# A scheduling priority for the evictions of pair products in a two-layer trunk kernel

## The chip, the core and the metric

The kernel runs on one core of a Trainium2 chip. A core has a matrix engine (TensorE, PE in the profile; its weight loads are shown apart as PEld), a vector engine (VectorE, DVE), an activation engine (ScalarE, ACT), a general engine (GpSimd, POOL) and an engine that here only issues loads (SyncE, SP). TensorE writes its results to eight PSUM banks; VectorE and ScalarE read them from there ("evict" them) into SBUF. The metric is device time in microseconds; smaller is better.

## The reference

Two layers of a streaming-encoder block on a sequence of 512 frames of width 1024. Cut to what matters:

```python
for i in range(2):
    h = rmsnorm(x, norm1_g[i])
    z = h @ w_in[i] + b_in[i]            # q,k,v,o,i,f / rq,rk,rv,rg / two gates
    y_m = sigmoid(mo) * head_layernorm(mlstm(...))
    y_r = silu(rg) * head_layernorm(retention(rope(rq), rope(rk), rv))
    merged = sigmoid(gm) * (y_m @ w_bm[i]) + sigmoid(gr) * (y_r @ w_br[i])
    x = x + merged @ w_out[i]
    h2 = rmsnorm(x, norm2_g[i])
    x = x + square(relu(h2 @ w_ff1[i] + b_ff1[i])) @ w_ff2[i] + b_ff2[i]
    h3 = rmsnorm(x, norm3_g[i])
    x = x + sigmoid(h3 @ w_pe_gate[i]) * (p[i] @ w_pe[i])
return rmsnorm(x, final_g)
```

The line with `w_ff2` is the second half of the channel mix. Everything is float32.

## The kernel before

**Numbers.** Each float32 matrix product is done as three products of reduced-precision parts. A tensor is split into a high part (ScalarE copies it, line 286) and a low part (VectorE subtracts, line 287), and `mm3` multiplies high by high, high by low and low by high. The splits of weights are the largest single use of both engines.

**Units.** The weights come in units, in the fixed order of `unit_list`. A whole unit ("T8", "V", "PE") is one raw tile `wr` of 128 x 1024, split into `wh` and `wl`; `t8` runs 24 matmuls of 512 columns on it. A pair unit ("PAIR") covers a 1024 x 256 block of weights by a seven-product scheme: instead of eight quarter products there are seven, P1 to P7, each with 12 matmuls of 256 columns on sums of weights and sums of activations. `run_pair` emits them in the order P1, P5, P6, P2, P3, P7; P4 is put off and emitted after P1 and P5 of the next unit, or at another place that calls `flush`. The seven products read four pieces of weights: A (P1 and P5), B (P2 and P6), C (P3 and P7) and D (P4). Pieces are prepared in the order A, C, B, D, and sums in between them (lines 421 and 424) form what D needs. Three pieces of 128 x 1024 and two of D are held at once, and four raw tiles.

**Banks.** In a pair P1, P6, P7 and P4 write the same PSUM bank (named a), P2 its own (b), and P5 and P3 share one (c). Each product is evicted before the next one of its bank begins. So P6 waits for the eviction of P1, P7 for that of P6, P4 for that of P7, and P3 for that of P5.

**Evictions.** In `pair_tiles`, which serves the retention's q, k and gate tiles and two branch gates, ScalarE copies P1 (line 548), P5 (550), P6 (554) and P4 (560) to two tiles y, and VectorE adds P2 (552), P3 (556) and P7 (558) to them. After P4's eviction `consume(y)` applies what follows. In `ff2`, the second half of the channel mix, VectorE adds all seven products to the residual x (lines 1398 and 1400). Names of banks in the profile: l1o33a is layer 1, `ff2` of block 3, part 3, bank a; l0r2o0a is layer 0, retention head 2, gate tile pair 0; l0r1brqa the q of head 1; l0bgm2a a branch gate. A split of weights is wh_A, wl_A and so on by its piece, wh and wl for a whole unit.

**What sets the order.** The program is written for a scheduler. It numbers the instructions in the order in which the program emits them and then plays the program through with its own estimate of every duration. Whenever an engine is free on that clock, it takes, among the instructions that are ready, the one with the lowest number. What comes out is a fixed list for each engine, which the engine then runs in that order, waiting where something isn't there. All engines are ordered so, TensorE too. The splits alone have an order of their own: `in_order` ties each to the one before. A product's splits are emitted ahead of it by `ready`, as many as `READY` says, up to five pieces from the unit's first, and so reach into the next unit. A split that is emitted before an eviction has the lower number.

Of the kernel before, what the change touches and what calls it, by code (L numbers as in the profile page):

```python
# [38 lines left out]
OP = mybir.AluOpType  # L39
# [12 lines left out]
S = 256  # L52
UN = 1024
LOOK = 2
WARM = 11
NTMP = 6
RAWS = 4
# [178 lines left out]
def build(ctx, tc, ins, out):  # L236
    nc = tc.nc
    ve, ac, gp, te = nc.vector, nc.scalar, nc.gpsimd, nc.tensor
# [40 lines left out]
    def ps(name):  # L279
        return psum.tile([P, T], F32, name=name, tag="ps")  # L280

    def tmp(name, dt=F32):
        return cur["tmp"].tile([P, T], dt, name=name, tag="t", bufs=cur["ntmp"])
# [147 lines left out]
    def ready(k):  # L431
        while at["prep"] < min(len(order), k + 1):
            prep_next()

    def unit(kind):
        n = next_unit()
        assert units[n][0] == kind, (units[n], kind)
        ready(place[n, 0] + LOOK)
        return units[n], *pieces.pop((n, 0))
# [6 lines left out]
    def t8(act, name):  # L446

        _, wh, wl = unit("T8")
        o = ps(name)
        for k in range(KT):  # L450
            s = slice(k * P, (k + 1) * P)
            mm3(o, wh[:, s], wl[:, s], act[0][k], act[1][k], k == 0, k == KT - 1)
            if k == 3:
                flush()
        return o
# [16 lines left out]
    def run_pair(name, act, done):  # L472

        n = next_unit()
        assert units[n][0] == "PAIR", units[n]
        bank = {}

        def product(x):
            w, half, j = PRODUCTS[x]
            ready(place[n, "A"] + READY[x])  # L480
            wh, wl = [a[:, half * Q:(half + 1) * Q] for a in pieces[n, w]]
            b = {"P2": "b", "P5": "c", "P3": "c"}.get(x, "a")
            first = x in ("P1", "P2", "P5")
            if first:
                bank[b] = ps(f"{name}{b}")
            o = bank[b][:, 0:S]
            for k in range(4):
                s = slice(k * P, (k + 1) * P)
                h, l = act[k](j)
                f, e = first and k == 0, k == 3  # L490
                te.matmul(o, wh[:, s], h, start=f, stop=False, skip_group_check=True)
                te.matmul(o, wh[:, s], l, start=False, stop=False, skip_group_check=True)
                cur["mm"] = te.matmul(o, wl[:, s], h, start=False, stop=e, skip_group_check=True)
            done(x, o)

        def last():
            product("P4")
            for w in PIECE:
                del pieces[n, w]

        product("P1")
        product("P5")
        flush()
        for x in ("P6", "P2", "P3", "P7"):
            product(x)
        later.append(last)

    def run_wide(name, act, done, mid=None):
# [4 lines left out]
        for x, u in TURNS:  # L513
# [9 lines left out]
            if first and u == 0:  # L523
                bank[b] = [ps(f"{name}{b}{t}") for t in range(2)]
            ready(place[n, (y, u)] + LOOK)
            wh, wl = pieces.pop((n, (y, u)))
# [10 lines left out]
            if u:  # L537
                for t in range(2):
                    done(x, t, bank[b][t])

    def pair_tiles(name, act, consume, y=None):

        y = y or [tmp(f"{name}y{d}") for d in range(2)]
        a, b = slice(0, S), slice(S, T)

        def done(x, o):
            if x == "P1":
                ac.activation(y[0][:, b], o, AF.Copy)
            elif x == "P5":
                ac.activation(y[1][:, a], o, AF.Copy)  # L550
            elif x == "P2":
                ve.tensor_tensor(y[0][:, b], o, y[0][:, b], OP.add)
            elif x == "P6":
                ac.activation(y[1][:, b], o, AF.Copy)
            elif x == "P3":
                ve.tensor_tensor(y[1][:, b], o, y[1][:, b], OP.add)
            elif x == "P7":
                ve.tensor_tensor(y[1][:, a], o, y[1][:, a], OP.add)
            else:
                ac.activation(y[0][:, a], o, AF.Copy)  # L560
                consume(y)

        run_pair(name, act, done)

# [141 lines left out]
    def bcol(i, n, k):  # L706
        o, _ = _B[n]
        return bc[:, i, o + k:o + k + 1]
# [184 lines left out]
    def big(name, dt):  # L893

        return [bpool.tile([P, T], dt, name=f"{name}{k}", tag="big", bufs=KT) for k in range(KT)]

    x = big("x0", F32)
# [5 lines left out]
    warm = ps("warm")  # L903
    for _ in range(WARM):
        te.matmul(warm[:, 0:P], ones, ones, start=True, stop=True)
# [13 lines left out]
    for i in range(L):  # L919
# [132 lines left out]
        def r_qk(h):  # L1052
            nm = f"l{i}r{h}"
            qk = qk_tiles(nm)

            def rope(a, bn):
                b = [bcol(i, bn, 2 * h + d) for d in range(2)]

                def consume(y):

                    for d in range(2):
                        u = tmp(f"{nm}{bn}u{d}")
                        w = tmp(f"{nm}{bn}w{d}")
                        ve.scalar_tensor_tensor(u, y[0], b[0], trig[d], OP.add, OP.mult)
                        ve.scalar_tensor_tensor(w, y[1], b[1], trig[1 - d], OP.subtract, OP.mult)
                        ve.tensor_tensor(u, u, w, (OP.add, OP.subtract)[d])
                        split(u, qk[2 * a][d], qk[2 * a + 1][d])

                return consume

            for a, bn in ((0, "brq"), (1, "brk")):
                pair_tiles(f"{nm}{bn}", xs, rope(a, bn))
            return qk
# [17 lines left out]
        def r_gates(h, w, gs):  # L1091

            def consume(g):
                for d in range(2):
                    ac.activation(g[d], g[d], AF.Silu, bias=bcol(i, "brg", 4 * h + 2 * w + d), scale=SIGN[d])
                    gs[2 * w + d] = g[d]

            pair_tiles(f"l{i}r{h}o{w}", xs, consume)
# [14 lines left out]
        def gm_gates(p):  # L1113
            def consume(g):
                for d in range(2):
                    ac.activation(g[d], g[d], AF.Sigmoid, bias=bcol(i, "bgm", 2 * p + d), scale=SIGN[d])
                    gm[2 * p + d] = g[d]

            pair_tiles(f"l{i}bgm{p}", xs, consume)
# [84 lines left out]
        for d in range(4):  # L1204
            o = t8(xa, f"l{i}m0z{d}") if d else oz
# [92 lines left out]
        for c in range(KT):  # L1298
            o = t8(yr, f"l{i}br0{c}")
# [20 lines left out]
        for c in range(KT):  # L1320
# [6 lines left out]
            o = t8(yr, f"l{i}br1{c}")  # L1327
# [13 lines left out]
        if i == L - 1:  # L1341
            x_pool = phase("x", act_side)
            whole = x_pool.tile([P, KT, T], F32, name=f"l{i}x", tag="x")
            x = [whole[:, c, :] for c in range(KT)]
        else:
            x = big(f"l{i}x", F32)
# [4 lines left out]
        for c in range(KT):  # L1351
            o = t8((mh, ml), f"l{i}wo{c}")
# [35 lines left out]
        def tile3(c):  # L1388
            n3.tile(c, x[c])

        def ff2(b, p):
            started = set()

            def add(q, o, op):
                y = x[2 * p + q // 2][:, (q % 2) * S:(q % 2 + 1) * S]
                if b == 0 and q not in started:
                    started.add(q)
                    ve.scalar_tensor_tensor(y, y, bcol(i, "bf2", 2 * p + q // 2), o, OP.add, op)
                else:
                    ve.tensor_tensor(y, y, o, op)  # L1400

            def done(x_, o):
                if x_ in ("P1", "P2"):
                    add(1, o, OP.add)
                elif x_ == "P5":
                    add(2, o, OP.subtract)
                elif x_ in ("P6", "P3"):
                    add(3, o, OP.subtract)
                elif x_ == "P7":
                    add(2, o, OP.subtract)  # L1410
                elif x_ == "P4":
                    add(0, o, OP.add)
                    if b == 3 and p == 3:
                        tile3(6)
                        tile3(7)
                if b == 3 and p and x_ in ("P6", "P7"):
                    tile3(2 * p - 2 + (x_ == "P7"))

            def parts(k):
                h, l = hid[b, k]  # L1420
                return lambda j: (h[:, j * S:(j + 1) * S], l[:, j * S:(j + 1) * S])

            run_pair(f"l{i}o{b}{p}", [parts(k) for k in range(4)], done)
# [19 lines left out]
        for u in range(2):  # L1443
            _, wh, wl = unit("PE")
            for c in range(4):
                o = ps(f"l{i}pe{u}{c}")
# [33 lines left out]
        for c in range(KT - LAST if last else KT):  # L1480
            o = t8(n3.act, f"l{i}pg{c}")
# [44 lines left out]
    for a, n in enumerate(nn):  # L1526
        for c in range(KT - LAST, KT):
            _, wh, wl = ws[c - KT + LAST]
            o = ps(f"pl{a}{c}")[:, :256]
# [140 lines left out]
```

## Time and profile before

| what | value |
|---|---|
| median of 3 runs | 2348.01 us (2347.84 to 2348.44) |
| profiled execution | 2347.49 us |
| its span, first to last instruction | 2345.8 us |
| TensorE busy | 2320.2 us, 99% |
| VectorE busy | 1722.9 us, 73% |
| ScalarE busy | 1218.9 us, 52% |
| weight splits, low part, VectorE: wl_A, one of 76 | 1220 ns |
| mean granted TensorE clock | 0.997 of full speed |

How to read it: TensorE's matmuls overlap, and their ends are modelled, so its busy time has no gap even where it starts a matmul late by less than the length of one. Its pace is better read from the distance between the starts of neighbouring matmuls. An idle time in brackets in a timeline is that of the engine before the instruction, and the name behind the arrow is what ended it. In the waits, "PE l1o33a L491 <- DVE l1x L1400" reads: TensorE, about to write bank l1o33a at line 491, waited for the VectorE instruction of line 1400 that wrote l1x.

### The profile page before, as it was taken

Reading aid. Unit: us, or ns where it says so; the run is one execution under the profiler, and the core shown is the slowest. Engines: PE = TensorE matmul, PEld = TensorE weight load, DVE = VectorE, ACT = ScalarE, POOL = GpSimd, SP = SyncE. Lnnn points to the kernel's source line nnn. Section 1 sums busy time; section 2 is a strip of 40 time slices with the busy share of each in tenths; the row PEclk is TensorE's granted clock in tenths of the full one; section 3 lists DMA queues with packets and bytes.
Section 4 is the critical chain, followed back from the end, with each engine's and each line's share of the span. In section 5 each row is a group of like instructions: output and inputs, shape, how many; then the busy total and the mean of one; then the engine's idle time right before and its main releaser. Section 6 shows DMA issues by size and latency. Waiting matters only on the chain. (4 is left out here: it accounts for less than half of the span.)

```text
span 2345.8 us, 35261 instructions
## 1 busy us (share of the span) xinstructions
PE 2320.2 (99%) x13660; PEld 2056.2 (88%) x13660; DVE 1722.9 (73%) x2658; ACT 1218.9 (52%) x1768; POOL 245.7 (10%) x369
## 2 busy tenths in 40 slices
PE   9999999999999999999999999999999999999998
PEld 7888899898898898899888888998989988998997
DVE  7878767895675577677878787778958656776785
ACT  6656444553554445446557564454536445445454
POOL 3111101100102100000321110000000020000012
PEclk9999999999999999999999999999999999999999
DMA  5666676667578667676775645434343542433431
GB/s 201 187 180 172 218 229 170 205 189 202 168 230 269 195 198 189 199 219 181 206 221 169 182 124 186 136 126 158 108 158 104 166 153 96 130 108 98 132 117 59
DMA packets 146631, 394.89 MB, mean 168 GB/s; under 512 B 15376, under 2 KB 18832, under 8 KB 146464
## 3 DMA queue, kind: packets, MB, share of 16 engines
q1 hardware_dynamic: 99952, 247.77, 32.0%
q0 software_dynamic: 31104, 117.45, 20.4%
q10 hardware_dynamic: 15408, 27.43, 3.3%
q8 instruction: 107, 1.75, 0.3%
q14 instruction: 60, 0.49, 0.1%
HBM read 373.71 MB, written 123.73 MB: 212 GB/s over the span
## 5 line engine op out<-in xcount | busy, mean ns | idle before, releaser
L286 ACT ACTIVATE wh<-wr 128x1024 fp32r<-128x1024 f32 (+1 forms) x223 | 232.2, 1044 | 276.5 <-issue 69.6
L287 DVE TENSOR_TENSOR wl<-wr,wh 128x1024 fp32r<-128x1024 f32 (+1 forms) x221 | 271.9, 1232 | 77.7 <-ACT wh L286 77.5
L286 ACT ACTIVATE wh_B<-wr 128x1024 fp32r<-128x1024 f32 x100 | 105.9, 1059 | 159.2 <-PE l0f L443 8.5
L287 DVE TENSOR_TENSOR wl_B<-wr,wh_B 128x1024 fp32r<-128x1024 f32 x100 | 121.9, 1219 | 32.5 <-ACT wh_B L286 32.3
L286 ACT ACTIVATE wh_D<-wr 128x512 fp32r<-128x512 f32 x76 | 48.0, 632 | 124.9 <-DVE wr L424 65.4
L286 ACT ACTIVATE wh_C<-wr 128x1024 fp32r<-128x1024 f32 x76 | 80.2, 1056 | 61.3 <-issue 9.2
L286 ACT ACTIVATE wh_A<-wr 128x1024 fp32r<-128x1024 f32 x76 | 79.9, 1052 | 54.7 <-PE l1f L443 9.0
L287 DVE TENSOR_TENSOR wl_C<-wr,wh_C 128x1024 fp32r<-128x1024 f32 x76 | 94.3, 1240 | 18.7 <-ACT wh_C L286 18.5
L287 DVE TENSOR_TENSOR wl_A<-wr,wh_A 128x1024 fp32r<-128x1024 f32 x76 | 92.7, 1220 | 17.3 <-ACT wh_A L286 17.3
L442 PE MATMUL l1f<-l1n2h,wh 128*128 128x512 f32 x256 | 99.8, 390 | 0.0
L442 PE MATMUL l0f<-l0n2h,wh 128*128 128x512 f32 x256 | 99.8, 390 | 0.0
L444 PE MATMUL l0f<-l0n2h,wl 128*128 128x512 f32 x256 | 99.7, 389 | 0.0
L444 PE MATMUL l1f<-l1n2h,wl 128*128 128x512 f32 x256 | 99.7, 389 | 0.0
L443 PE MATMUL l1f<-l1n2l,wh 128*128 128x512 f32 x256 | 99.6, 389 | 0.0
L443 PE MATMUL l0f<-l0n2l,wh 128*128 128x512 f32 x256 | 99.6, 389 | 0.0
L287 DVE TENSOR_TENSOR wl_D<-wr,wh_D 128x512 fp32r<-128x512 f32 x76 | 52.4, 689 | 33.2 <-ACT wh_D L286 31.7
L421 DVE TENSOR_TENSOR wr<-wr,wr 128x512 f32<-128x512 f32 x76 | 52.1, 686 | 14.6 <-DMA wr<-wpairs 13.1
L444 PEld LDWEIGHTS l0f<-l0n2h,wl 128*128 128x128 f32 x256 | 48.0, 188 | 10.2
L444 PEld LDWEIGHTS l1f<-l1n2h,wl 128*128 128x128 f32 x256 | 48.1, 188 | 10.1
L443 PEld LDWEIGHTS l1f<-l1n2l,wh 128*128 128x128 f32 x256 | 48.1, 188 | 9.8
L442 PEld LDWEIGHTS l0f<-l0n2h,wh 128*128 128x128 f32 x256 | 48.1, 188 | 9.8
L442 PEld LDWEIGHTS l1f<-l1n2h,wh 128*128 128x128 f32 x256 | 48.1, 188 | 9.7
(5625 smaller groups left out, 8357.9 us busy)
## 6 DMA issues: line engine op xcount, KB each, us to landing
wr<-wstream SPq DMA_DIRECT2D x219, 512.0 KB, 4.2
wr<-wpairs SPq DMA_DIRECT2D x228, 256.0 KB, 2.8
wr<-wwide SPq DMA_DIRECT2D x24, 512.0 KB, 4.0
s0t<-wwide POOLq DMA_DIRECT2D x5, 1024.0 KB, 7.8
s4t<-wwide POOLq DMA_DIRECT2D x5, 1024.0 KB, 9.0
s12t<-wwide POOLq DMA_DIRECT2D x5, 1024.0 KB, 8.1
s16t<-wwide POOLq DMA_DIRECT2D x5, 1024.0 KB, 8.5
s1t<-wpairs POOLq DMA_DIRECT2D x4, 1024.0 KB, 6.7
```

What stands on the lines that cost most here:

```text
L286: a = ac.activation(hi_ap, src, AF.Copy)
L287: return a, ve.tensor_sub(lo_ap, src, hi_ap.bitcast(F32))
L421: ve.tensor_tensor(raws[n, "B"][:, Q:], kept.pop((n, "A"))[:, Q:], r[:, :Q], OP.add)
L442: te.matmul(o, sh, mh, start=first, stop=False)
L443: te.matmul(o, sh, ml, start=False, stop=False)
L444: cur["mm"] = te.matmul(o, sl, mh, start=False, stop=last)
```

## The change

`tc.high_priority(250)` is a context of the scheduler: instructions emitted inside it get a number that is lower by 250. The change puts the evictions of a pair's products inside such a context, in `pair_tiles` and in `ff2`. An eviction that is ready then comes before any ready instruction of the same engine that was emitted up to 250 instructions earlier, splits of weights among them. What follows an eviction, `consume(y)` and the norm's work, keeps its number. The instructions themselves and what they depend on are the same.

```diff
+AHEAD = 250
...
+    def ahead():
+
+        return tc.high_priority(AHEAD)
+
     def pair_tiles(name, act, consume, y=None):
...
         def done(x, o):
+            with ahead():
+                evict(x, o)
+            if x == "P4":
+                consume(y)
+
+        def evict(x, o):
             if x == "P1":
                 ac.activation(y[0][:, b], o, AF.Copy)
...
             else:
                 ac.activation(y[0][:, a], o, AF.Copy)
-                consume(y)
...
             def add(q, o, op):
                 y = x[2 * p + q // 2][:, (q % 2) * S:(q % 2 + 1) * S]
-                if b == 0 and q not in started:
-                    started.add(q)
-                    ve.scalar_tensor_tensor(y, y, bcol(i, "bf2", 2 * p + q // 2), o, OP.add, op)
-                else:
-                    ve.tensor_tensor(y, y, o, op)
+                with ahead():
+                    if b == 0 and q not in started:
+                        started.add(q)
+                        ve.scalar_tensor_tensor(y, y, bcol(i, "bf2", 2 * p + q // 2), o, OP.add, op)
+                    else:
+                        ve.tensor_tensor(y, y, o, op)
```

## The prediction

> **What bounds the kernel now.** I read the page first, then TensorE's waits, then the timelines of VectorE and ScalarE at the longest of them. Section 1 of the page:
>
> ```profile
> span 2345.8 us, 35261 instructions
> PE 2320.2 (99%) x13660; PEld 2056.2 (88%) x13660; DVE 1722.9 (73%) x2658; ACT 1218.9 (52%) x1768; POOL 245.7 (10%) x369
> ```
>
> TensorE is busy for all but 25.6 us of the span (2345.8 - 2320.2). The change touches no matmul, so about 1.1% is the most that any reordering of the other engines can show as idle time removed. The work is therefore to see which of those 25.6 us are waits for an eviction. TensorE's waits, longest first (who, for whom: us in total, times, longest):
>
> ```profile
> PE l0r2o1a L491 <- ACT wh_A L286: 3.4, 1, 3.4
> PE l1o33a L491 <- DVE l1x L1400: 1.6, 1, 1.6
> PE l0o33a L491 <- DVE l0x L1400: 1.3, 1, 1.3
> ...
> PE l0r0o0a L491 <- DVE l0r0o0y L558: 1.2, 1, 1.2
> PE l1r0o0a L491 <- DVE l1r0o0y L558: 1.2, 1, 1.2
> ...
> PE l0r1brqa L491 <- DVE l0r1brqy L558: 1.0, 1, 1.0
> ...
> PE l0o12a L491 <- DVE l0x L1400: 0.7, 1, 0.7
> ...
> PE l1r2o0a L491 <- ACT l1r2o0y L548: 0.5, 1, 0.5
> ...
> PE l0r2o0a L491 <- ACT l0r2o0y L548: 0.4, 1, 0.4
> ```
>
> Eight of these nine rows are released by one of the evictions that the change moves (L548, L558, L1400): 1.6 + 1.3 + 1.2 + 1.2 + 1.0 + 0.7 + 0.5 + 0.4 = 7.9 us. The largest is released by a split. So the profile has something for this change to win, but it is small: 7.9 us are 0.34% of 2348.0. I call 0.2% (4.7 us) the least that counts as a difference from no change.
>
> **The change, part by part.** It adds and removes no instruction, no DMA and no wait in the code; it gives the seven evictions of every pair a better place in the order in which VectorE and ScalarE take ready work. SyncE's loads and POOL's sums keep their places; a raw buffer comes free later only by as much as a split is delayed. A pair is 84 matmuls and 7 evictions, so 250 instructions reach back over two pairs, past every split that can still be open. On ScalarE, 52% busy, four evictions per pair also pass other activations; I cost that at nothing, since its idle half covers them.
>
> *P7's eviction before P4 (five places).* P4 writes the PSUM bank that P7's eviction reads. The worst place of its kind in layer 0, VectorE's rows and then TensorE's (start us, us, engine, line, operation; idle time before it in brackets):
>
> ```profile
> 412.74 1.22 DVE L287 TENSOR_TENSOR wl_A<-wr,wh_A 128x1024 fp32r<-128x1024 f32 x1
> 413.88 0.42 DVE L552 TENSOR_TENSOR l0r0o0y<-l0r0o0b,l0r0o0y 128x256 f32<-128x256 f32 x1
> 414.21 0.41 DVE L556 TENSOR_TENSOR l0r0o0y<-l0r0o0c,l0r0o0y 128x256 f32<-128x256 f32 x1
> 414.54 1.21 DVE L287 TENSOR_TENSOR wl_C<-wr,wh_C 128x1024 fp32r<-128x1024 f32 x1
> 415.67 0.42 DVE L558 TENSOR_TENSOR l0r0o0y<-l0r0o0a,l0r0o0y 128x256 f32<-128x256 f32 x1
> ...
> 414.74 0.28 PE L444 MATMUL l0r1s<-l0r1qh,l0r1kl 128*128 128x256 f32 x1
> 416.24 0.36 PE L491 MATMUL l0r0o0a<-l0xnh,wh_D 128*128 128x256 f32 x1 [1.22 <-DVE l0r0o0y L558]
> 416.43 0.28 PE L492 MATMUL l0r0o0a<-l0xnl,wh_D 128*128 128x256 f32 x1
> ```
>
> A split of 1.21 us (wl_C) stands directly ahead of the 0.42 us eviction for which TensorE is stopped. With the eviction first, it starts 1.13 us earlier (415.67 - 414.54) at the least, and more where it also passes wl_A. The loss at TensorE is larger than the wait: between starts lie 1.50 us where the neighbouring 256-column matmuls lie 0.12 apart, so 1.38, and the next distance is 0.19 instead of 0.12; together 1.45 for a wait of 1.22, or 0.23 more per place. Five waits of this kind (l1o33a, l0o33a, l0r0o0a, l1r0o0a, l0r1brqa) sum to 6.3 us, with 5 x 0.23 = 1.15 to 7.4 us. At l1o33a the blocker is of the same sort:
>
> ```profile
> 2282.96 1.99 DVE L287 TENSOR_TENSOR wl<-wr,wh 128x1024 fp32r<-128x1024 f32 x1
> 2284.88 0.41 DVE L1400 TENSOR_TENSOR l1x<-l1x,l1o33a 128x256 f32<-128x256 f32 x1
> ```
>
> The bounds are 0 (the eviction was not yet ready when the scheduler took the split) and 7.4; in the rows one split alone costs as much as the wait, so I take 7.3.
>
> *P1's eviction before P6 (two places, l0r2o0 and l1r2o0).* Here the eviction is ScalarE's, behind splits of the retention scores. Layer 0, where loads were late too; ScalarE's rows:
>
> ```profile
> 598.58 0.63 ACT L286 ACTIVATE l0r3vh<-l0r3vr 128x512 fp32r<-128x512 f32 x1 [2.83 <-DMA l0r3vr<-rv_spill]
> ...
> 602.69 1.04 ACT L286 ACTIVATE wh_A<-wr 128x1024 fp32r<-128x1024 f32 x1
> 604.01 1.03 ACT L286 ACTIVATE l0r3ph<-l0r3p 128x384 fp32r<-128x384 f32 x3 [0.28 <-DVE l0r3p L770]
> 604.95 0.36 ACT L548 ACTIVATE l0r2o0y<-l0r2o0a 128x256 f32<-128x256 f32 x1
> ```
>
> and three stretches of this place (TensorE, weight loads, VectorE, ScalarE, POOL busy with counts; granted clock; DMA share and GB/s):
>
> ```profile
> 600.40:603.70 3.30, 0.00 (x0) 0.00 (x0) 2.40 (x5) 2.45 (x4) 0.00 (x0) 0.81 1.01 398
> 603.70:609.40 5.70, 5.26 (x23) 4.97 (x24) 4.16 (x10) 2.89 (x8) 0.00 (x0) 0.51 0.35 113
> 609.40:620.00 10.60, 10.60 (x92) 10.60 (x91) 6.53 (x9) 6.17 (x11) 0.00 (x0) 1.00 0.34 106
> ```
>
> This is the kernel's only long stop: no matmul for 3.4 us, then 23 matmuls in 5.70 us at a granted clock of 0.51, which at the next stretch's pace (10.60 / 92 = 0.115 us) would have taken 2.65; so 3.4 + 3.05 = 6.4 us. TensorE had P6 of l0r2o0 left and lacked only P1's eviction for it; the scheduler, which orders TensorE's list too, had for that reason put the first matmuls of l0r2o1, with the late wh_A, ahead of P6. That eviction can pass at least wh_A and l0r3ph, 604.95 to 602.69, a gain of 2.3 us; the late load ahead of them (2.83 us) isn't touched. I take 2.1 here, with 0 and 6.4 as ends, and for layer 1 its wait of 0.5 with the 0.23 from above, 0.7. Together 2.8.
>
> The Trainium skill (TensorE: Matmul & The Clock Gate, Part 1, on the HAM clock gate) says that TensorE falls to half its clock after an idle window of about 3.4 us and needs about as long of steady work to come back. The row of 0.51 agrees. By that rule an eviction 2.3 us earlier would cut this stop below the window and save the slow stretch too, about 4.3 us for this place and 2338.8 in the end; I stay with 2.1, since only one such stop is in the trace.
>
> *P5's eviction before P3, channel mix (six places, o00, o10, o20 of both layers).* First and last of the six, TensorE's rows:
>
> ```profile
> 842.08 0.28 PE L493 MATMUL l0o00b<-l0hh,wl_B 128*128 128x256 f32 x1
> 842.37 0.38 PE L491 MATMUL l0o00c<-l0hh,wh_C 128*128 128x256 f32 x1
> ...
> 2166.05 0.28 PE L493 MATMUL l1o20b<-l1hh,wl_B 128*128 128x256 f32 x1
> 2166.36 0.39 PE L491 MATMUL l1o20c<-l1hh,wh_C 128*128 128x256 f32 x1
> ```
>
> Starts lie 0.29 and 0.31 us apart instead of 0.12, about 0.18 lost at each. I count this as 0, because of the next item: a microsecond later the same pairs hand over to a split that will be late.
>
> *The splits that are passed.* Every eviction moved ahead delays the splits behind it by 0.33 us (413.88 to 414.21 above). That is covered where the split is early. The tightest kind outside the channel mix is a whole unit like this one, which ends at 336.81 and is first read at 338.07, 1.26 us later, or three evictions:
>
> ```profile
> 335.60 1.21 DVE L287 TENSOR_TENSOR wl<-wr,wh 128x1024 fp32r<-128x1024 f32 x1
> ...
> 338.07 0.39 PE L444 MATMUL l0bm<-l0ymh,wl 128*128 128x512 f32 x1
> ```
>
> It is not covered for the first split of the second pair in a row in the channel mix (o01, o11, o21, both layers: six places). VectorE, then TensorE:
>
> ```profile
> 927.93 1.22 DVE L287 TENSOR_TENSOR wl_A<-wr,wh_A 128x1024 fp32r<-128x1024 f32 x1
> 929.07 0.41 DVE L1400 TENSOR_TENSOR l0x<-l0x,l0o10b 128x256 f32<-128x256 f32 x1
> 929.40 0.41 DVE L1400 TENSOR_TENSOR l0x<-l0x,l0o10c 128x256 f32<-128x256 f32 x1
> ...
> 929.20 0.38 PE L493 MATMUL l0o11a<-l0hh,wl_A 128*128 128x256 f32 x1
> ```
>
> The split ends at 929.15 and TensorE reads it 0.05 us later; two evictions that now come after it would come before it. Cost: 0 if neither was ready in time, 2 x 0.33 = 0.66 per place if both were, 0 to 4.0 us over six. P2's product (bank b) is older by one product than P3's (bank c), so one is nearly sure and the other open: I take 0.5 per place, 3.0 us.
>
> *l0o12a* (0.7) I leave as it is: its eviction stands behind a split that itself waited long for its data:
>
> ```profile
> 942.25 1.23 DVE L287 TENSOR_TENSOR wl_B<-wr,wh_B 128x1024 fp32r<-128x1024 f32 x1 [2.78 <-ACT wh_B L286]
> ```
>
> Sum: -7.3 - 2.8 + 3.0 = -7.1 us. The profiled execution took 2347.49 us, its span 2345.8 and 1.7 around it; the median of the three runs, 2348.01, is 0.5 above it. I put the sum on the median: **2341.0 us**, 0.30% faster.
>
> **The rivals.**
> *The priority finds little to pass.* The scheduler orders by its own clock. Where it believes that the split could start before the product was done, a better rank changes nothing, as at l0o12a, where VectorE stood 2.78 us at a split that the scheduler must have thought ready. For it also: l0r1brqa is waited for in layer 0 only, though both layers run the same code, so that wait hangs on how a load happened to land. Against it: at l0r0o0 VectorE was busy without a gap from 412.74 to 416, so split and eviction were both ready. Half of the 10.1 us won and the 3.0 paid leave 2.1: 2345.9 us, within 0.2%.
>
> *The queue behind an eviction stops.* VectorE and ScalarE run their lists in order. Where the scheduler's TensorE is ahead of the real one, P7's eviction stands at the head waiting for its product, and the next pair's wl_A behind it. That split would then end 0.41 + 1.22 = 1.6 us after P7, just when TensorE wants it. TensorE can start only the first matmuls of the next product meanwhile. Each pair so caught costs up to 1.6 us, and there are 76 pairs; 7.1 / 1.6, between four and five, eat the forecast's gain, and from eight on the kernel is slower by over 0.2%. With nine it comes to 2341.0 + 14.4 = 2355.4, which I take. For it: VectorE does already wait for products at evictions,
>
> ```profile
> DVE l1x L1400 <- PE l1o13a L493: 2.2, 2, 2.0
> ```
>
> Against it: a scheduler that takes only what is ready by its clock would have issued wl_A, which is ready before P7 ends, first. The Trainium skill (TensorE: Matmul & The Clock Gate, on the engine queue depths) calls the queues of ScalarE and VectorE strict FIFO; the split wl_B that held back a ready eviction at 942.25 agrees, and the rule speaks for this rival's mechanism without giving its size.
>
> **How the numbers follow.** Forecast 0.57: the blockers are seen in the rows, and small delays of splits are mostly covered. Little to pass: 0.25. A stopped queue: 0.18. So faster by over 0.2%: 0.57, within 0.2%: 0.25, slower: 0.18. The forecast's own range is 2334 (7.4 + 7.1 won, nothing paid) to 2343.3. The 8 in 10 range takes in the second case whole and the third up to nine caught pairs, 2334 to 2355.
>
> **What would show it.** Right: the five waits for L558 and L1400 gone from TensorE's waits; L548 of l1r2o0 ahead of the split l1r3ph; new or longer waits of 0.3 to 0.7 us for wl_A at o01, o11, o21; VectorE's and ScalarE's busy time and counts unchanged. Wrong: TensorE waiting for wl_A at many pairs; or the long stop near 600 us kept, moved, or doubled, since one such stop (6.4 us) is as large as the whole forecast.

## The result and the profile after

The changed kernel is slower: 2358.34 us median (2355.49 to 2362.18, five runs) against 2348.01 (2347.78 to 2349.22, five runs), a ratio of 1.0043 with an interval of 1.003 to 1.0056. The profiled execution took 2359.73 us. Section 1 of its page:

```profile
span 2358.0 us, 35261 instructions
PE 2324.5 (99%) x13660; PEld 2058.7 (87%) x13660; DVE 1723.5 (73%) x2658; ACT 1218.6 (52%) x1768; POOL 244.1 (10%) x369
```

Counts and busy times are those of before (VectorE 1723.5 for 1722.9, ScalarE 1218.6 for 1218.9); the span is 12.2 us longer. So no engine has more to do; something waits. In the changed file the lines of the prediction stand 1 to 11 lower: 287 and 288 are the splits, 422 and 425 the sums between pieces, 492 to 494 a pair's matmuls, 559, 561, 567 and 569 the evictions of `pair_tiles`, 1409 and 1411 those of `ff2`. TensorE's waits after (who, for whom: us in total, times, longest):

```profile
PE l0r2o1a L492 <- ACT wh_A L287: 3.4, 1, 3.4
PE l0o11a L492 <- DVE l0x L1411: 2.4, 2, 1.7
PE l0o02a L492 <- DVE l0x L1409: 2.3, 1, 2.3
PE l0o21a L492 <- DVE l0x L1411: 1.9, 2, 1.6
PE l0o33a L492 <- DVE l0x L1411: 1.7, 1, 1.7
PE l1o33a L492 <- DVE l1x L1411: 1.5, 1, 1.5
...
PE l0r1brqa L492 <- DVE l0r1brqy L569: 1.0, 1, 1.0
...
PE l1o11a L494 <- DVE wl_A L288: 0.8, 1, 0.8
PE l1o21a L494 <- DVE wl_A L288: 0.8, 1, 0.8
PE l0o11a L494 <- DVE wl_A L288: 0.8, 1, 0.8
PE l0o21a L494 <- DVE wl_A L288: 0.8, 1, 0.8
...
PE l1r0o0a L492 <- DVE l1r0o0y L569: 0.2, 1, 0.2
PE l0r0o0a L492 <- DVE l0r0o0y L569: 0.2, 1, 0.2
```

The reader is to see three things. The waits at r0o0 went from 1.2 to 0.2. Four waits of 0.8 for wl_A are new, as forecast. And three places that were not in the list before stand right behind its longest wait: l0o11, l0o02, l0o21, all in layer 0's channel mix, all waits for an eviction that was given priority.

Where the time came from shows best by stage. A stage here lasts from the first matmul of one bank's first tile to that of the next named one, in TensorE's timeline of one profiled execution each. The channel mix is the stretch from the first matmul of o00a to that of the next norm:

| stage | before | after |
|---|---|---|
| layer 0, pairs, l0r1brqa to the first of l0wo | 362.32 | 361.78 |
| layer 1, pairs, l1r1brqa to the first of l1wo | 355.18 | 354.21 |
| layer 0 channel mix, block 0 | 83.55 | 86.87 |
| block 1 | 84.57 | 87.87 |
| block 2 | 83.76 | 87.77 |
| block 3 to the norm | 47.06 | 47.59 |
| layer 0 channel mix, sum | 298.94 | 310.10 |
| layer 1 channel mix, sum | 296.97 | 299.66 |

Layer 0's channel mix loses 11.2 of the 12.2 us; layer 1's, the same code, 2.7; the two pair stages win 1.5. VectorE's waits within layer 0's channel mix name what is new, before and then after:

```profile
DVE wr L421 <- DMA wr<-wpairs: 4.1, 3, 1.8
```

```profile
DVE wr L422 <- DMA wr<-wpairs: 18.8, 8, 4.4
```

VectorE now stands for 18.8 us, eight times, at the sum of line 422, waiting for weights to land. (At the splits wl_B it stands less than before, 4.1 us for 8.9.) One such place in full, at the second pair of block 1. After the change, VectorE's timeline (start us, us, engine, line, operation; idle time before it in brackets) and TensorE's next row:

```profile
931.84 1.22 DVE L288 TENSOR_TENSOR wl_A<-wr,wh_A 128x1024 fp32r<-128x1024 f32 x1
...
941.40 0.69 DVE L422 TENSOR_TENSOR wr<-wr,wr 128x512 f32<-128x512 f32 x1 [3.79 <-DMA wr<-wpairs]
942.00 0.69 DVE L288 TENSOR_TENSOR wl_D<-wr,wh_D 128x512 fp32r<-128x512 f32 x1
942.61 0.41 DVE L1411 TENSOR_TENSOR l0x<-l0x,l0o11a 128x256 f32<-128x256 f32 x1
```

```profile
943.08 0.38 PE L492 MATMUL l0o11a<-l0hh,wh_C 128*128 128x256 f32 x1 [1.69 <-DVE l0x L1411]
```

Before, the same stretch of VectorE's list:

```profile
934.12 0.69 DVE L287 TENSOR_TENSOR wl_D<-wr,wh_D 128x512 fp32r<-128x512 f32 x1
934.81 0.42 DVE L1400 TENSOR_TENSOR l0x<-l0x,l0o11a 128x256 f32<-128x256 f32 x1
935.14 1.22 DVE L287 TENSOR_TENSOR wl_A<-wr,wh_A 128x1024 fp32r<-128x1024 f32 x1
...
936.61 0.68 DVE L421 TENSOR_TENSOR wr<-wr,wr 128x512 f32<-128x512 f32 x1
```

Two things differ. The sum now stands in the list ahead of wl_D and of the eviction of P6 (l0o11a), and what it reads isn't there for 3.79 us; before it stood behind both and behind wl_A, and did not wait. TensorE's P7 needs the bank that this P6 eviction empties, so it stops 1.69 us. The other two long waits are of the same kind: at 864.66 the sum waits 4.37 us ahead of the eviction for l0o02a, at 1029.20 it waits 3.72 ahead of that for l0o21a.

Why the weights are late: the load that lands last here was issued at 933.08 after, at 929.18 before. Loads issued in these narrow windows, with POOL's sum transfer (1024 KB) that was in flight beside them, KB each and us from issue to landing; after, then before:

```profile
s15t<-wpairs POOLq DMA_DIRECT2D x1, 1024.0 KB, 12.6
wr<-wpairs SPq DMA_DIRECT2D x1, 256.0 KB, 8.2
```

```profile
s15t<-wpairs POOLq DMA_DIRECT2D x1, 1024.0 KB, 11.6
wr<-wpairs SPq DMA_DIRECT2D x1, 256.0 KB, 2.8
```

And when POOL issued, after and then before:

```profile
932.32 0.91 POOL L332 DMA_DIRECT2D s15t<-wpairs  x1 [13.38 <-PE l0o10a L494]
```

```profile
929.30 0.91 POOL L331 DMA_DIRECT2D s15t<-wpairs  x1 [13.56 <-PE l0o10a L493]
```

Before, the load went out 0.12 us ahead of POOL's transfer and took 2.8 us. After, it went out 0.76 us behind it and took 8.2. Counted from the block's first matmul (920.01 before, 923.21 after) POOL issues at 9.3 and 9.1, so it is the load that moved, from 9.2 to 9.9. It is issued when its raw tile comes free: 0.02 to 0.03 us behind the end of the split wl_A of the pair o11 (start 927.93 in the rows of the prediction, 931.84 above, 1.22 us each). That split started 7.9 us into the block before and 8.6 after, so split and load moved by the same 0.7. Splits keep their order among themselves, and the one ahead of wl_A is piece D's: wl_D started at 926.05 before, 931.24 after, 6.0 and 8.0 us into the block, since l0hl, an eviction and other work now come ahead of it. Block 2 shows the same: the load behind its wl_A goes out 0.08 us ahead of POOL's transfer and takes 2.7 us before, 0.81 behind it and 8.2 us after. In block 0 the load that the sum waits for goes out 0.83 behind; there the sum stood ahead of the eviction before the change too, and only the load is new. Layer 1 has none of POOL's transfers in this stage, and its 42 loads there land in a median of 2.7 us in both kernels.

### The profile page after: what moved, and what is told of

Same layout as the page of the kernel before. It is cut to its first block, busy times and chain, and to the rows that moved or that the text cites. A ratio compares the mean times of both kernels' runs of the same rounds, so it can differ in the third digit from the quotient of the medians.

```text
span 2358.0 us, 35261 instructions
## 1 busy us (share of the span) xinstructions
PE 2324.5 (99%) x13660; PEld 2058.7 (87%) x13660; DVE 1723.5 (73%) x2658; ACT 1218.6 (52%) x1768; POOL 244.1 (10%) x369
## 3 DMA queue, kind: packets, MB, share of 16 engines
q0 software_dynamic: 31104, 117.45, 20.2%
## 4 chain that ended last, share of the span: by engine, by line
PE 87%; DVE 7%; DMA 2%; issue 2%; ACT 1%; POOL 0%; SPq 0%; DVEq 0%; ACTq 0%; POOLq 0%
PE l0f L443 2%; PE l1f L443 2%; PE l0f L444 2%; PE l1f L444 2%; PE l1f L445 2%; PE l0f L445 2%; DMA wr<-wpairs 1%; PE l0br L443 1%; PE l1br L443 1%; PE l1br L445 1%; PE l0br L444 1%; PE l1br L444 1%; PE l0br L445 1%; DVE wl_B L288 1%; PE l0bm L443 1%
## 5 line engine op out<-in xcount | busy, mean ns | idle before, releaser
L444 PEld LDWEIGHTS l0f<-l0n2l,wh 128*128 128x128 f32 x256 | 48.1, 188 | 9.7
```

The costliest lines, as they stand in the source:

```text
L444: te.matmul(o, sh, ml, start=False, stop=False)
```

## The experiments

Ratios are to the kernel before on the same chip, with 95% intervals. "Layer 0" is the sum of the four channel-mix stages of layer 0 in the profiled execution, worked out as above.

| kernel | median us | ratio | layer 0 |
|---|---|---|---|
| before | 2348.0 to 2349.7 | 1 | 298.9 |
| after | 2358.34 | 1.0043 [1.003, 1.0056] | 310.1 |
| e1_ff_only | 2361.27 | 1.0048 [1.0033, 1.0063] | 308.3 |
| e2_pairs_only | 2346.77 | 0.9988 [0.9979, 0.9997] | 298.5 |
| e3_no_sums_after | 2340.29 | 0.9956 [0.9941, 0.9971] | 299.6 |
| e4_no_sums_before | 2337.89 | 0.9945 [0.9928, 0.9961] | 298.5 |
| e5_sum_behind_C | 2370.81 | 1.0094 [1.0079, 1.0109] | 312.3 |
| e6_D_first_too | 2356.07 | 1.0035 [1.0022, 1.0048] | 305.4 |
| e8_sum_on_pool | 2362.40 | 1.0054 [1.0037, 1.0071] | 311.5 |
| e10_pairs_D_first | 2346.50 | 0.9988 [0.9979, 0.9998] | 298.7 |
| e11_after_sums_later | 2364.55 | 1.0065 [1.005, 1.008] | 317.7 |
| e13_before_sums_later | 2353.38 | 1.002 [1.0011, 1.003] | 306.1 |
| e15_before_sums_earlier | 2352.05 | 1.0014 [1.0005, 1.0024] | 300.6 |
| e14_D_chain_first | 2346.03 | 0.9988 [0.9978, 0.9997] | 299.6 |
| e16_D_chain_alone | 2347.87 | 0.9993 [0.9984, 1.0002] | 297.8 |
| e17_pairs_and_D_chain | 2345.42 | 0.9981 [0.9973, 0.999] | 298.0 |

### Which half of the change: e1 and e2

```diff
 # e1_ff_only, against after: pair_tiles as before
-            with ahead():
-                evict(x, o)
+            evict(x, o)
 # e2_pairs_only, against after: ff2 as before
-                with ahead():
-                    if b == 0 and q not in started:
+                if b == 0 and q not in started:
...
```

> Priority in ff2 alone, none in pair_tiles. Theory A (all of the loss lies in the channel mix: stage distances between the profiles before and after grow by 11.2 us in layer 0's channel mix and by 2.7 in layer 1's, while the pair stages shrink by 2.0): 2348.0 + 12 to 14 = 2360 to 2362, with a spread of some us from run to run. Rival (the changes of the pair stages shift when loads and sums collide later, so that the loss needs both): under 2355.

> Priority in pair_tiles alone, none in ff2. Theory A: the pair stages' gain without the loss, 2348.0 - 2.0 = 2346.0, 2345 to 2347, spread as small as before's 0.3 us. Rival (both parts needed): 2348 or more, or a spread of some us.

The loss is all with `ff2`: priority there alone gives 2361.27 and 308.3 us in layer 0's channel mix, priority in `pair_tiles` alone 2346.77 and 298.5. The pairs' half is worth about 3 us against before on the same chip (2349.72; 0.7 to 4.9 by the interval), not the seven that my forecast put on the whole.

### Are late loads the cause: e3 and e4

```diff
 # e3_no_sums_after on after, e4_no_sums_before on before, the same edit
-                sums[g, x] = tc.dram_tile([n, P, w], F32, name=f"s{index[g]}{x}")
+                pass
...
-        return given[g, x] if x in GIVEN else sums[g, x]
+        return given[g, x if x in GIVEN else {"t1": "B11", "t3": "B22", "t2": "B12"}[x]]
...
-        dma = gp.dma_start(flat(block(g, x)), flat(block(g, MADE[x][a])), max_dma_last_dim=4096, **kw)
-
-        tc.add_manual_dep(dma.ins, cur["mm"].ins.name, SYNC, reason="pace of the sums")
```

> The changed kernel without POOL's sums of weight blocks in DRAM: the loads that would read a sum read the first given block instead, so loads keep their number and size, the sums' own transfers are gone, and the output isn't the reference's. To be set against the next run. Theory B (layer 0 loses more than layer 1 because POOL's sums make its loads land late, and VectorE stands at the sum of line 422 with evictions queued behind): the loss against the same edit of the kernel before falls from 10 to 1 to 4 us, and layer 0's channel mix costs as much as layer 1's. Rival C (the new order itself costs it, whatever the loads do): the difference stays near 10 us.

> The kernel before with the same edit (no sums in DRAM, first given block read instead, output not the reference's); the baseline for the run before. Both theories: TensorE's long stop near 600 us may go too, since it waits for loads, so 2338 to 2348.

Without POOL's transfers the two lists differ by 2.4 us instead of 10.3, and by 1.2 in layer 0's channel mix instead of 11.2. So about nine tenths of that stage's loss need POOL's transfers. In e3 the pairs' loads of this stage land in a median of 2.9 us. These two runs take all of that traffic away; that it acts through late loads is for the runs below, which keep it. The change's own list has a remaining price of 1 to 2 us, which fits the four waits for wl_A.

### Moving the sum that stands: e5 and e8

```diff
 # e5_sum_behind_C, against after
-            ve.tensor_tensor(raws[n, "B"][:, Q:], kept.pop((n, "A"))[:, Q:], r[:, :Q], OP.add)
+            late = ve.tensor_tensor(raws[n, "B"][:, Q:], kept.pop((n, "A"))[:, Q:], r[:, :Q], OP.add)
+            tc.add_manual_dep(late.ins, cur["prep"][1].ins.name, ORDER, reason="sum behind the split of C")
 # e8_sum_on_pool, against after
-            ve.tensor_tensor(raws[n, "B"][:, Q:], kept.pop((n, "A"))[:, Q:], r[:, :Q], OP.add)
+            gp.tensor_tensor(raws[n, "B"][:, Q:], kept.pop((n, "A"))[:, Q:], r[:, :Q], OP.add)
```

> The changed kernel, with VectorE's sum of line 422 (which waits for the late load of a pair's piece B) tied behind the split of piece C in VectorE's list, so that fewer evictions and splits are queued behind it. Theory D (the place of the sum in the list is what hurts: VectorE stands at it 18.8 us in layer 0's channel mix, with ready evictions behind): most of the loss goes, 2358 falls to 2348 to 2351. Rival E (the load itself is late, because the splits that free its raw buffer are late; whatever waits for it, TensorE does in the end): 2355 or more, the wait moves to wl_B.

> The changed kernel with the sum of line 422 done by POOL instead of VectorE: nothing on VectorE's list waits for that load any more except the split wl_B. Theory D: the waits of TensorE for line 1411 in layer 0's channel mix go, 2348 to 2352, unless POOL's slower sum makes wl_B late. Rival E: wl_B is late instead, with the evictions queued behind it as before, 2355 or more.

Neither helps: e5 takes 2370.81 us and is slower than after, e8 takes 2362.40 and is level with it (the intervals overlap; 311.5 us in the stage for 310.1). If the sum's place in VectorE's list were the whole cause, taking it from there should have helped. It did not, because the late weights then stop the next instruction that needs them. VectorE in e8, where the sum has left the engine:

```profile
943.58 1.23 DVE L288 TENSOR_TENSOR wl_C<-wr,wh_C 128x1024 fp32r<-128x1024 f32 x1 [6.50 <-ACT wh_C L287]
944.72 0.42 DVE L1411 TENSOR_TENSOR l0x<-l0x,l0o11c 128x256 f32<-128x256 f32 x1
```

It stands 6.50 us at wl_C, again with evictions behind it. The first half of its load went out 0.80 us behind POOL's transfer and took 9.9 us. In e5 the same split waits, for 3.33 us, and the tile that the delayed sum still reads comes free later, so the next loads start later still: the one at this place goes out 3.4 us behind POOL's.

### Freeing D's raw tile: e6 and e10

```diff
 # e6_D_first_too on after, e10_pairs_D_first on e2_pairs_only
-            in_order("prep", *split(r[:, :w], *out_))
+            with ExitStack() as st:
+                if x == "D":
+                    st.enter_context(tc.high_priority(AHEAD))
+                in_order("prep", *split(r[:, :w], *out_))
```

> The changed kernel, with the split of piece D in the same priority context as the evictions, so that its raw buffer comes free earlier again (in the profile after, wl_D of the pair o10 of layer 0 starts 2.2 us later against the pair than in the profile before, and the next loads are issued right behind it). Rival E (late loads): most of the loss in layer 0 goes, 2349 to 2352. Theory D (place in the list): little changes, 2355 to 2360.

> Priority in pair_tiles and for the split of D, none in ff2. If late loads cost something in the kernel before too (rival E), this is faster than priority in pair_tiles alone: 2343 to 2346 beside its 2346.8. Theory D: the same as that run, 2346 to 2348.

D's split in the priority brings after from 310.1 to 305.4 in layer 0's channel mix; block 0 is back at 83.61, with no wait at that sum, blocks 1 and 2 are not (86.73 and 87.44). The whole time, 2356.07, can't be told from after's (the intervals overlap). At block 1 wl_D started 7.7 us into the block, hardly earlier than after's 8.0: the sum that forms D, line 425, kept its number and was itself passed by the evictions. wl_A started at 8.6, as in after, so the load went out 0.76 us behind POOL's transfer again and took 8.3 us. e10 shows that the same edit does no harm with the pairs' half (2346.50).

### Moving POOL's transfers: e11, e13 and e15

```diff
 # e11_after_sums_later on after, e13_before_sums_later on before
-        tick(units[n][0])
+        if units[n][0] != "PAIR":
+            tick(units[n][0])
...
+        tick("PAIR")
 # e15_before_sums_earlier, against before: paced by P3's last matmul, not P7's
-        tc.add_manual_dep(dma.ins, cur["mm"].ins.name, SYNC, reason="pace of the sums")
+        tc.add_manual_dep(dma.ins, cur.get("pace", cur["mm"]).ins.name, SYNC, reason="pace of the sums")
...
+            if x == "P3":
+                cur["pace"] = cur["mm"]
```

> The changed kernel with POOL's transfers for the sums of weight blocks let go one to two products later in each pair (after P5 and the put-off P4 of the pair instead of at its start), some 3 to 4 us. Theory F (the evictions delay the split that frees a raw buffer, the next load is issued 0.7 to 1.2 us later and so just behind the start of POOL's transfer, and lands after 6 to 8 us instead of 2.7): the load at 9.9 us after the block's start slips in front of the transfer again, the loss in layer 0's channel mix falls from 11 to 2 to 5 us, 2349 to 2353. Rival G (a late load costs wherever the transfer stands, since some load always meets it): 2356 or more.

> The kernel before with the same later sums; the control. Theory F: layer 0's channel mix as before or a little better, 2346 to 2350. Rival G: 2348 as well, but then the run above does not come near it.

> The kernel before, with no priority anywhere, and POOL's transfers for the sums let go one product earlier in each pair (at the end of P3 instead of P7, 1.4 us). Theory F: the load that is issued at 9.2 us after a block's start, 0.1 to 0.2 us ahead of the transfer, now comes behind it and lands late: layer 0's channel mix loses 5 to 12 us without any priority, 2353 to 2360, with some us from run to run. Rival H (the evictions' place in VectorE's list is needed for the loss): within 2 us of the kernel before.

e11 does not heal the change: 317.7 in the stage, with VectorE waiting 20.2 us at the sum. The load of the disputed place in block 1 (929.51) is ahead of POOL's transfer (934.04) again, takes 3.8 us, and nothing waits for it; but the load for the pair after it (935.27) goes out 1.23 behind and takes 7.8, and TensorE's long waits are now at l0o12 and l0o22 (3.2 and 3.1 us). Part of the 317.7 is another thing: the last block costs 54.63, and e13, which has the same later transfers and no priority, loses as much there (55.17 for 47.06). Its first three blocks are as before or better, so e13 says nothing on the disputed place. e15 is the useful one: it makes the late load meet a list without any priority. In block 1 the load issued at 933.30 goes out 1.2 us behind POOL's (932.13) and lands as late as after's:

```profile
wr<-wpairs SPq DMA_DIRECT2D x1, 256.0 KB, 7.6
```

VectorE in e15:

```profile
938.94 0.42 DVE L1404 TENSOR_TENSOR l0x<-l0x,l0o11a 128x256 f32<-128x256 f32 x1
939.28 1.22 DVE L287 TENSOR_TENSOR wl_A<-wr,wh_A 128x1024 fp32r<-128x1024 f32 x1
...
940.94 0.69 DVE L423 TENSOR_TENSOR wr<-wr,wr 128x512 f32<-128x512 f32 x1
943.54 1.23 DVE L287 TENSOR_TENSOR wl_C<-wr,wh_C 128x1024 fp32r<-128x1024 f32 x1 [1.91 <-ACT wh_C L286]
```

The eviction of l0o11a is done by 939.36, before the sum; the block takes 83.63 us. So a 7.6 us load costs nothing here, and the same holds in block 2 (7.8 us, 83.88). The stage as a whole is 1.6 us longer than before, and block 0 alone loses 1.9 (85.49 for 83.55). There the sum stands ahead of the eviction for l0o02a without any priority, in the list of before too (859.37 and 861.08, with no wait at the sum), and now its load is late:

```profile
865.59 0.69 DVE L423 TENSOR_TENSOR wr<-wr,wr 128x512 f32<-128x512 f32 x1 [3.97 <-DMA wr<-wpairs]
...
867.20 0.47 DVE L1402 SCALAR_TENSOR_TENSOR l0x<-l0x,bc,l0o02a 128x256 f32<-128x256 f32 x1
```

TensorE then waits 1.7 us for that eviction; after the change it waits 2.3 at the same place. With e3 this makes a table of two by two for layer 0's channel mix: a list without priority with loads on time 298.5 (e4), with late loads 300.6 (e15); after's list with loads on time 299.6 (e3), with late loads 310.1. The new list alone costs 1.2 us, the late loads alone nothing where the eviction stands ahead of the sum, the two together more than eleven. Theory F of the expectation, that the late load is enough, missed (2352.05, expected 2353 to 2360): the eviction must stand behind the sum as well.

### Undoing the cause inside the change: e14

```diff
 # e14_D_chain_first, against after: e6's edit, and the sum that forms D
-            ve.tensor_tensor(r[:, :Q], r[:, :Q], r[:, Q:], OP.add)
+            with tc.high_priority(AHEAD):
+                ve.tensor_tensor(r[:, :Q], r[:, :Q], r[:, Q:], OP.add)
```

> The changed kernel with the sum that forms piece D (line 425) and the split of D both in the priority context, so that their raw buffer comes free earlier than in the earlier run, which gave the split alone and moved it by 0.3 us only. Theory F: in blocks where the next loads get in front of POOL's transfer the loss goes, 2349 to 2354; the loss that is left is that of wl_A and of blocks where they don't. Rival H: 2356 or more in spite of earlier loads.

With both steps of D's chain in the priority the whole loss is gone: 2346.03, 299.6 in the stage. All evictions still have their priority. VectorE at the place shown above:

```profile
931.59 0.68 DVE L425 TENSOR_TENSOR wr<-wr,wr 128x512 f32<-128x512 f32 x1
...
932.79 0.41 DVE L1415 TENSOR_TENSOR l0x<-l0x,l0o11a 128x256 f32<-128x256 f32 x1
```

The sum (here line 425) still stands ahead of the eviction, as in after, but its load was issued at 925.70, 1.3 us ahead of POOL's (927.02), and landed in time:

```profile
wr<-wpairs SPq DMA_DIRECT2D x1, 256.0 KB, 2.7
```

The four waits for wl_A are gone too: at block 1 wl_A starts 6.5 us into the block, after's at 8.6. Late loads as such are not gone: VectorE still stands 10.6 us at this sum in the stage, six times, for 4.1 before. At 939.25 it stands 2.33 us there, and behind it TensorE waits 0.9 us at l0o12, where before, with VectorE 2.78 us at wl_B, it waited 0.7. So the length of VectorE's waiting is no measure of the loss.

### What the chain is worth by itself: e16 and e17

e16 is before with e14's two edits alone; e17 is e2 with them.

> Kernel before with one addition: the sum that forms D and D's split get the priority (250 instructions); no eviction has any. Theory (the loss came only from evictions passing D's chain in the channel mix, and an earlier D chain is worth something by itself because D's raw buffer comes free sooner): the block l0o10 is issued and costed as before or better, its four channel-mix stages of layer 0 sum to 297 to 300 us (298.9 before), time 2344 to 2349. Rival (what the two additions recovered in the earlier run needed the evictions ahead as well): the D chain now passes evictions of the channel mix that TensorE waits for, the four stages cost 2 to 6 us more than before, time 2350 to 2354.

> The priority for the pairs' evictions alone (none for the channel mix's sums), and for the sum that forms D and D's split. Theory: the pair stages give the 1 to 2 us that the priority gave there in every kernel that had it, and the D chain what it gives alone; so 1 to 2 us below the kernel with the D chain alone, 2343 to 2347. If the channel mix's priority is worth its name once the D chain is no longer passed, then the kernel with all three (2346.0) stands at least 1 us below this one; if it is worth nothing, this one is level with it or faster.

The chain alone is level with before (0.9993, the interval holds 1): its own worth is not shown, so e14's 3 us below before are not shown to come from it. e17 has the lowest median of the kernels that compute the reference (e3 and e4 don't), 2345.42, 4.2 us below before on its chip; it beats before and after, but its interval overlaps those of e2, e10 and e14. It has no priority in `ff2`, and e14, which has it, is not faster (2346.03). So the priority in `ff2` is worth nothing that can be measured, even where it does no harm.

## Why the prediction was wrong

Forecast 2341.0, in the range 2334 to 2355; the time is 2358.34, slower and outside.

**The step that failed** stands in one sentence of the change part by part: "a raw buffer comes free later only by as much as a split is delayed", costed at nothing. As far as it goes it held: in block 1 the split wl_A, which frees the raw tile, came 0.7 us later, and the load was issued 0.7 us later. What the step left out is that a load's landing is not its issue plus a constant: 0.7 us later meant behind POOL's transfer, and 8.2 us instead of 2.8. The prediction had listed POOL's queue and SyncE's as keeping their places, which they did; what changed was which of them came first. The second half of the error is the place of the line 422 sum. I looked at splits that evictions pass, and not at what then stands in front of the next eviction when loads are late. Together they make nearly 10 of the 11.2 us of layer 0's channel mix, by difference (1.9 are its two waits for wl_A, and 0.5 came back at P3; e3 and e4 also leave 1.2 of 11.2 without POOL's transfers), and nothing in the sum stood for them.

**P7's eviction before P4 (7.3 forecast).** The prediction calls l0r0o0 (1.2) the worst place of its kind in layer 0; by its own list that is l0o33a (1.3). It was right at l0r0o0 and l1r0o0: the eviction now stands ahead of wl_D and wl_A, and the wait is 0.2. VectorE after:

```profile
413.19 0.42 DVE L569 TENSOR_TENSOR l0r0o0y<-l0r0o0a,l0r0o0y 128x256 f32<-128x256 f32 x1
413.52 0.68 DVE L288 TENSOR_TENSOR wl_D<-wr,wh_D 128x512 fp32r<-128x512 f32 x1
```

Two of the 6.3 us of waits went. At l0r1brqa the 1.0 stayed: VectorE stood 3.68 us at the sum for a load, then ran wl_C, and only then the evictions.

```profile
385.17 0.69 DVE L422 TENSOR_TENSOR wr<-wr,wr 128x512 f32<-128x512 f32 x1 [3.68 <-DMA wr<-wpairs]
385.78 1.22 DVE L288 TENSOR_TENSOR wl_C<-wr,wh_C 128x1024 fp32r<-128x1024 f32 x1
...
387.25 0.42 DVE L569 TENSOR_TENSOR l0r1brqy<-l0r1brqa,l0r1brqy 128x256 f32<-128x256 f32 x1
```

At o33 of both layers they stayed too (1.7 and 1.5 for 1.3 and 1.6); a whole unit's wl is still directly ahead of the eviction. Layer 1, VectorE after:

```profile
2295.49 1.98 DVE L288 TENSOR_TENSOR wl<-wr,wh 128x1024 fp32r<-128x1024 f32 x1
2297.39 0.41 DVE L1411 TENSOR_TENSOR l1x<-l1x,l1o33a 128x256 f32<-128x256 f32 x1
```

The rival in which the priority finds little to pass holds at these three places: the list still puts a split first, so on the scheduler's clock the product was not done. That this is its reason was not tried.

**P1's eviction before P6 (2.8 forecast).** The long stop of layer 0 is kept: TensorE waits 3.44 us for wh_A, and the following 5.70 us run at a granted clock of 0.50. That stretch of after (TensorE, weight loads, VectorE, ScalarE, POOL busy with counts; granted clock; DMA share and GB/s):

```profile
603.55:609.25 5.70, 5.53 (x25) 5.38 (x26) 4.20 (x9) 3.03 (x8) 0.00 (x0) 0.50 0.34 123
```

ScalarE's list moved the eviction ahead of two of three pieces of l0r3ph and not ahead of wh_A, 604.38 for 604.95:

```profile
602.63 1.04 ACT L287 ACTIVATE wh_A<-wr 128x1024 fp32r<-128x1024 f32 x1
603.95 0.52 ACT L287 ACTIVATE l0r3ph<-l0r3p 128x384 fp32r<-128x384 f32 x1 [0.28 <-DVE l0r3p L780]
604.38 0.37 ACT L559 ACTIVATE l0r2o0y<-l0r2o0a 128x256 f32<-128x256 f32 x1
```

Of the 2.1 nothing came, since TensorE's list still has the matmul for wh_A first. In layer 1 the wait of 0.5 is gone. What a shorter stop would do to the clock stays open: in every run the stop is 3.4 to 3.8 us, or gone (e3, e4). The prediction's price for such a shorter stop does not add up either: 2.1 for the eviction and 3.05 for the slow stretch make 5.2 us and 2337.9, not 4.3 and 2338.8.

**wl_A delayed (3.0 forecast).** Right in mechanism, and near in size: at o11 and o21 of both layers, none at o01. TensorE at l1o11, after:

```profile
2096.72 0.28 PE L493 MATMUL l1o11c<-l1hl,wh_A 128*128 128x256 f32 x1
2097.77 0.39 PE L494 MATMUL l1o11a<-l1hh,wl_A 128*128 128x256 f32 x1 [0.77 <-DVE wl_A L288]
```

Starts lie 1.05 apart instead of 0.12, so 0.93 at each of four places, 3.7 us for 3.0.

**P5's eviction before P3 (0 forecast).** Won at all six places: starts lie 0.12 apart where they lay 0.29 to 0.31, about 0.18 each, 1.1 us. TensorE at the first of them, after:

```profile
841.95 0.28 PE L494 MATMUL l0o00b<-l0hh,wl_B 128*128 128x256 f32 x1
842.06 0.28 PE L492 MATMUL l0o00c<-l0hh,wh_C 128*128 128x256 f32 x1
```

**The slower rival** had the sign and half of the picture: VectorE's list does stop, and what TensorE needs stands behind. But what stands at the head is a sum that waits for a load, and what is held back is an eviction; the rival had an eviction at the head and a split behind.

Not settled: layer 1's 2.7 us. Two waits for wl_A make 1.9 of it, and three P3 places give 0.5 back; the rest, about 1.3, is little more than the 1.1 by which block 0 of layer 1 alone varies between kernels without priority in `ff2` (82.45 in before, 83.55 in e2 and e4).

## What to carry to other kernels

Before giving some work priority, list what frees the buffers that the next loads wait for, and give that chain the same priority; here a split that came 0.7 us later moved a load behind a large transfer. In a fixed list, the instruction to fear is not the long one but the one that waits for a DMA: whatever stands behind it, with priority or not, waits too. A wait shown as "TensorE waits for an eviction" tells who is late, not that its rank is the reason; look at what that engine did in the microseconds before.

## What the hardware showed beyond what was expected

A 256 KB load took 2.8 us when issued 0.12 us ahead of one of POOL's 1024 KB transfers for the sums, 2.7 when 1.3 ahead, 7.6 and 8.2 when 1.2 and 0.76 behind it. In these four cases it is close to a step at the moment of issue; one more load in after (1020.20) went out 0.05 us behind such a transfer and still landed in 3.0. Not every load behind such a transfer is hit so hard: of the layer 0 channel-mix loads in after (256 and 512 KB) whose landing the trace gives, the 34 issued while one was in flight land in a median of 4.9 us, the other 17 in 3.5. The Trainium skill (DMA: Bandwidth & Descriptors, Queues, rings and completion order) says that each DMA engine takes turns, packet by packet, between the queues for which it has work. The rows agree that the two queues share the engines, since the load behind POOL's transfer is not held until that lands (8.2 against 12.6 us) and is held far beyond its 2.8; no run here shows the packets' turns themselves.

The only long stop of the kernel, 3.4 us with a granted clock of 0.50 after it, also comes from this traffic. In e4 it is not in TensorE's waits, and the stage from l0r1brqa to the first of l0wo takes 355.17 us for 362.32. My forecast had looked for a gain there in the order of ScalarE's work.
